# The residual h as eight tiles, operands of the next attention pair ahead of v, four raw weight buffers in the front, caches inside block 0's projections

## The chip, the core and the metric

The kernel runs on one core of a Trainium2 chip. The core has TensorE (PE, matmuls and transposes), VectorE (DVE), ScalarE (ACT), GpSimd (POOL) and SyncE (SP, which here issues every DMA, in one queue and in order). Each engine works its instructions off in the order in which the program has them, and engines wait for one another by semaphores. The metric is the device time of one execution in microseconds; lower is better. The time of a kernel is the median of some runs.

## What is computed

One step of a one-layer encoder over 2048 prompt tokens and 32 sample tokens, D = 1024, all in float32:

```python
z = rmsnorm(h, g_attn) @ w_in                      # 3072 columns: q, k, v of groups A and B
oa = diff_core(qa, ka, va, t5_bias, chunk_mask, lam)  # A: 4 heads, two softmaxes of 64 dims, values of 128
ob = band_core(qb, kb, vb, clip_bias, band_mask)      # B: 8 heads of 64, own chunk and the 8 before
h = h + concat([rmsnorm(oa, subln_g) * 0.8, rmsnorm(ob, out_norm_b)]) @ w_out
c = rmsnorm(h, g_mlp)
h = h + jnp.square(jax.nn.relu(c @ w_up)) @ w_down    # 4096 wide
h = h + jax.nn.sigmoid(h @ w_ple_gate) * (p @ w_ple_proj)
y = rmsnorm(h, g_final)
```

For the 32 sample tokens, keys and values of 128 cached positions (cache_a_k, cache_a_v, cache_b_k, cache_b_v) stand ahead of the new ones. The new keys and values are outputs too.

## The kernel before, in words

**Precision.** A float32 product is made of three fast ones: each operand is split into a high part and the rest (`split`, L194: the high part by ACT or DVE, the rest by POOL or DVE), and `mm3` (L215) issues high·high, high·rest and rest·high. So each weight is loaded raw, cast by ACT and subtracted by POOL (`wunit`, L205). A raw weight takes one of `nraw` buffers of a ring `rawp`; in the front these are two.

**Tokens** stand in four blocks (0 to 3) of 512, 544 (512 and the 32 sample tokens), 512 and 512. Most tensors are kept transposed, 128 features by tokens. What doesn't fit in SBUF is kept in scratch tensors in HBM: qS, kS and vS (split q, k, v), oT (attention's output), hS (the residual h), rS and rB (norms), uS, cS and eS (for the last two blocks' MLP).

**Order of the program** (`run`, L1417). The tile framework allocates buffers, sets all waits and orders the instructions of each engine by a planner: it keeps the program's order as priority and fills an engine's gaps with later work that is ready by its own simulation. Work far behind in the text can so run between earlier work; the MLP of block 0, for instance, fills the gaps of the second attention stage.

1. `prep` of blocks 0 and 1 (norm and transposes), then `proj` (L392): for group A, block 0, then block 1, values first, then q and k for each head pair. Each k tile is also turned back for the output by transposes (`knat`, L478), which wait in a list `late` until the next matmuls of the same call are issued, and at the latest until the end of the call. `setup` (L262) makes the lambda and the bias tables, woven into block 0's projections at steps 0, 8 and 10.
2. `attn_a` (L545) for the query pairs (0, 1), then block 1's projections, `bands`, `caches` (L502: cached keys transposed, split and written to kS, cached values to vS), then the pairs (2, 3) and the sample (8). For each head g a bias tile ba, the keys ka (and ks for the sample) are loaded, then for each pair `attn_a_pair` (L564): q is loaded, scores, softmax, then per four key tiles v is loaded, the weights transposed and multiplied. ba, ka and ks have one buffer in this stage, q and v two.
3. Projections for group B, `attn_b` (L708) of the same form with keys, values and bias loaded per head, and `proj` of blocks 2 and 3 for group A.
4. `weave2` with ONP: the norms of group B's outputs for blocks 0 and 1 (`onorm`) run beside these projections, at steps counted by ONP. Then `attn_a` for the pairs (4, 5) and (6, 7).
5. `outproj` and `cnorm` for blocks 0 and 1, then `mlp` for block 0 and for block 1 (L1556 to L1574): h is loaded from hS into one tile of 8 x 544 columns, each of 16 chunks of the hidden width adds into it (L993), and one DMA stores it to hS at the end (L1574). Beside block 1's MLP runs `side` (L1537): 29 steps in all, `oload` and `outproj` of blocks 2 and 3 (25 with a norm) and four of `xnorm3`, five at a time from chunk 8 on (SIDE).
6. Blocks 2 and 3 together by one step of Strassen's scheme, seven products instead of eight: `uphase` (L1101) with sums of weights ws (L1084) and of activations, then `dphase` (L1177) with weight tiles wd (six buffers). Beside dphase the gates and final norms of blocks 0 and 1 run (`gate`, `final`), behind it those of 2 and 3 (`gatepair`).

At the seam from 5 to 6 the pools of the MLP are closed and those of the up phase are opened in the same part of SBUF: hh (h of blocks 2 and 3), tw (split weights), tr (raw weights), then t2 with 18 buffers, some of which lie where h of block 1 lay.

Of the kernel before, what the change touches and what calls it, by code (L numbers as in the profile page):

```python
# [19 lines left out]
P = 128  # L20
# [63 lines left out]
ONP = (28, 1, 6)  # L84
# [4 lines left out]
SIDE = (8, 5)  # L89
# [70 lines left out]
class Kern:  # L160
    def __init__(self, tc, a):
        self.tc = tc
        self.nc = tc.nc
        self.a = a
        self.nt = 4
        self.nraw = 2

# [94 lines left out]
    def setup(self, cp, wk, ps):  # L262
# [15 lines left out]
        self.rb = self.dram([8, 768], F32, "rb")  # L278
        yield
# [28 lines left out]
        yield  # L308

# [82 lines left out]
    def proj(self, half, grp, acts, sg, mm, tp, vs=range(2), gs=range(4)):  # L392
# [7 lines left out]
        for c in vs:  # L400
# [3 lines left out]
            for b in half:  # L404
                aH, aL = acts[b]
                for c0, n in toks(b):
# [8 lines left out]
                    )  # L415
                    raw = sg.tile([P, 256], F32, tag="vraw", bufs=2, name="vraw")
# [18 lines left out]
        late = []  # L435
        for g in gs:
            gi = 4 * grp + g
            for kind in range(2):
                col = base + 512 * kind + P * g
                wh, wl = self.wunit(W[:, col : col + P].rearrange("(k p) c -> p k c", p=P), [8, P])  # L440
                for b in half:
# [5 lines left out]
                    for s0, n in SUBS[b]:  # L447
# [8 lines left out]
                        while late:  # L456
                            late.pop(0)()
# [38 lines left out]
                    if grp == 0 or b in (1, 3):  # L496
                        late.append(knat)
        while late:
            late.pop(0)()
        yield  # L500

    def caches(self, sg, tp):  # L502
        nc, a = self.nc, self.a
        for grp in range(2):
            nh, dv = (4, 128) if grp == 0 else (8, 64)
            ck = a["cache_a_k"] if grp == 0 else a["cache_b_k"]
            cv = a["cache_a_v"] if grp == 0 else a["cache_b_v"]
            kn = sg.tile([P, 512], F32, tag="kn", bufs=2, name="ckn")
            self.dma(kn, ck)
            tps = tp.tile([P, 4, P], F32, tag="mm", name="ctp")  # L510
            for g in range(4):
                nc.tensor.transpose(tps[:, g], kn[:, P * g : P * g + P], self.ident)
            hi = sg.tile([P, BLK], F32R, tag="qh", bufs=2, name="ckh")[:, :512]
            lo = sg.tile([P, BLK], F32R, tag="ql", bufs=2, name="ckl")[:, :512]
            tf = tps.rearrange("p a b -> p (a b)")
            nc.scalar.activation(hi, tf, AF.Copy)
            nc.vector.tensor_tensor(lo, tf, hi.bitcast(F32), op=ALU.subtract)
            for i, t in enumerate((hi, lo)):
                for g in range(4):
                    self.dma(  # L520
                        self.kS[4 * grp + g, i, :, SP : SP + PAST], t[:, P * g : P * g + P]
                    )
            for c in range(2):
                raw = sg.tile([P, 256], F32, tag="vraw", bufs=2, name="cvr")
                self.dma(raw, cv[:, 256 * c : 256 * c + 256])
                hl = sg.tile([P, nh // 2, 2, dv], F32R, tag="vhl", bufs=2, name="cvhl")
                r3 = raw.rearrange("p (h d) -> p h d", d=dv)
                self.split(hl[:, :, 0], hl[:, :, 1], r3, "dve", "pool")
                self.dma(
                    self.vS[grp][SP : SP + PAST, 512 * c : 512 * c + 512],  # L530
                    hl.rearrange("p a b d -> p (a b d)"),
                )
# [12 lines left out]
    def attn_a(self, js, pool, ps_s, ps_t, ps_o):  # L545
        nc = self.nc
        last = 8 in js
        nk = 256 * (max(j for j in js if j < 8) + 1)
        for g in range(4):
            ba = self.bias_a(pool, g)  # L550
            kt = pool.tile([P, 2, 1024 if self.small else SP], F32R, tag="ka", bufs=1 if self.small else 2, name="ka")
            if last:
                ks = pool.tile([P, 2, PAST + SS], F32R, tag="ks", bufs=1, name="ks")
            for hl in range(2):
                src = self.kS[g, hl].rearrange("(m r) c -> r m c", m=2)
                for c0 in range(0, nk, 1024):
                    c1 = min(c0 + 1024, nk)
                    self.dma(kt[64 * hl : 64 * hl + 64, :, c0:c1], src[:, :, c0:c1])
                if last:
                    self.dma(ks[64 * hl : 64 * hl + 64], src[:, :, SP:KC])  # L560
            for j in js:
                self.attn_a_pair(g, j if j < 8 else None, kt if j < 8 else ks, ba, pool, ps_s, ps_t, ps_o)

    def attn_a_pair(self, g, j, kt, ba, pool, ps_s, ps_t, ps_o):  # L564
# [8 lines left out]
        q = self.load_q(pool, g, t0, nq, (0, 1))  # L573
        ws = []
        for qi, t in enumerate(tiles):
# [132 lines left out]
    def attn_b(self, js, pool, ps_s, ps_t, ps_o):  # L708
        nc = self.nc
# [3 lines left out]
        for h in range(8):  # L713
            gi, m = 4 + h // 2, h % 2
            bb = self.bias_b(pool, h)
            kt = pool.tile([P, KBW], F32R, tag="kb", bufs=2, name="kbt")
            for hl in range(2):
                src = self.kS[gi, hl, 64 * m : 64 * m + 64]
                self.dma(kt[64 * hl : 64 * hl + 64, : ke - kb], src[:, kb:ke])
                if last:  # L720
                    self.dma(kt[64 * hl : 64 * hl + 64, ke - kb : ke - kb + PAST + SS], src[:, SP:KC])
            nv = (ke - kb) // P
            v = pool.tile([P, KBW // P + 1, P], F32R, tag="vb", bufs=2, name="vbt")
            self.dma(
                v[:, :nv],
                self.vS[1][kb : kb + nv * P, P * h : P * h + P].rearrange("(k p) c -> p k c", p=P),
            )
            if last:
                self.dma(v[:, nv], self.vS[1][SP : SP + PAST, P * h : P * h + P])
                self.dma(v[:SS, nv + 1], self.vS[1][SP + PAST : KC, P * h : P * h + P])  # L730
            for j in js:
                if j < 8:
                    self.attn_b_pair(h, j, kt, v, kb, bb, pool, ps_s, ps_t, ps_o)
                else:
                    self.attn_b_pair(h, None, kt, v, SP - (ke - kb), bb, pool, ps_s, ps_t, ps_o)

    def attn_b_pair(self, h, j, kt, v, kb, bb, pool, ps_s, ps_t, ps_o):
# [7 lines left out]
        q = self.load_q(pool, gi, t0, nq, (m,))  # L745
# [4 lines left out]
        for qi, t in enumerate(tiles):  # L750
# [31 lines left out]
            for x0 in range(0, len(kts), 4):  # L782
# [7 lines left out]
                for a0, na, kn in groups:  # L790
# [5 lines left out]
                    nc.vector.tensor_tensor(l_, s_, h_.bitcast(F32), op=ALU.subtract)  # L796
        o = ps_o.tile([P, 256], F32, tag="o", name="ob")
# [165 lines left out]
    def mlp_down(self, ch, nf, blocks, us, st, wk, mm):  # L963
# [3 lines left out]
        for dh in range(nf):  # L967
# [6 lines left out]
            for d in range(nd):  # L974
                dd = nd * dh + d
                for b in blocks:
                    h = st[b][0]
                    for s0, sn in SUBS[b]:
# [13 lines left out]
                        hv = h[:, dd, s0 : s0 + sn]  # L992
# [184 lines left out]
    def dphase(self, h, pool, md):  # L1177
# [35 lines left out]
        for m, sq, so, outs in plan:  # L1213
# [11 lines left out]
            for d in range(4):  # L1225
                for q, op in outs:
                    i, t = int(q[0]) - 1, int(q[1]) - 1
                    hv = h[2 + t][:, 4 * i + d, :512]
# [86 lines left out]
    def gatepair(self, h, up, act, pool, md, mg, lag):  # L1315
# [4 lines left out]
        for b in HALVES[1]:  # L1320
            hs[b] = [act.tile([P, 8, 512], F32R, tag="act", name=n) for n in ("hH", "hL")]
            for i, k in enumerate(order[b]):
                self.split(hs[b][0][:, k], hs[b][1][:, k], h[b][:, k, :], "act", "pool" if i % 4 == 1 else "dve")
        wg, wq = {}, {}
        for i in range(8 + lag):
            for d, b in ((i, 2), (i - lag, 3)):
# [19 lines left out]
                for s0, sn in ((0, 256), (256, 256)) if (d, b) == (7, 3) else ((0, 512),):  # L1346
# [15 lines left out]
                    self.sigate(up, pg, pq, h[b][:, d, t], sn < 512)  # L1362
                yield d, b

    def turned(self, h, c0, tn, q, ps, up, acc):
        nc = self.nc
        yp = ps.tile([P, 512], F32, tag="mm", name="yp")
        for k in range(4):
            nc.tensor.transpose(yp[:tn, P * k : P * k + P], h[:, 4 * q + k, c0 : c0 + tn], self.ident)
# [47 lines left out]
    def run(self):  # L1417
        tc, nc, a = self.tc, self.nc, self.a
        with ExitStack() as top:
# [22 lines left out]
            sg = opened(s12, "sg", 2)  # L1442
            self.consts(cp)
# [229 lines left out]
```

## Time and profile before

| | us |
|---|---|
| median of 3 runs | 3195.66 |
| lowest and highest | 3192.92, 3199.41 |
| the profiled execution | 3189.55 |
| its span, first to last instruction | 3187.7 |
| mean granted clock of TensorE | 0.977 of full |

The profile is of one execution. Busy time counts an engine's own instructions; issue of DMAs and waits are not in it. Waits are put down to what ended last before the waiting instruction started. "L993" is line 993 of the kernel; a tile's name is given as output<-input. A DMA's line is L173 throughout, so its tiles tell which one it is. PE's matmuls overlap, and gaps under some 0.1 us don't show as idle time. The granted clock is full speed or half.

### The profile page before, as it was taken

What the parts mean: (1) busy time and instruction counts of PE and PEld (TensorE: products, weight loads), DVE (VectorE), ACT (ScalarE), POOL (GpSimd) and SP (SyncE); (2) the same over time, 40 slices, a digit from 0 to 9 for tenths busy, and PEclk for the clock granted to TensorE, in tenths of its full rate; (3) what the DMA queues carried; (4) which work ended last, traced back from release to release, by engine and by line L of the source; (5) the groups of instructions that cost most, each with busy time, mean ns of one, the idle gap of its engine ahead of it and who ended that gap; (6) DMA issues with size and microseconds to landing.
All of it is one profiled execution on the core that took longest, in us unless ns stands there. A gap on an engine that the chain in (4) does not pass through costs nothing. (4 is left out here: it accounts for less than half of the span.)

```text
span 3187.7 us, 51326 instructions
## 1 busy us (share of the span) xinstructions
PE 3002.7 (94%) x17399; PEld 2626.0 (82%) x17399; DVE 1785.7 (56%) x4008; ACT 1774.0 (56%) x3809; POOL 1795.1 (56%) x2512
## 2 busy tenths in 40 slices
PE   7898888999999999999999999998799999999997
PEld 6787788889887987888888999888688878878776
DVE  5364655544345545667686652246466665845844
ACT  5465657766566656667676643334244454534454
POOL 7574563543334555556564465667465567767561
PEclk9998999999999999999999999999899999999999
DMA  8986868877777846555555343465544476756721
GB/s 245 285 235 180 226 182 243 245 228 229 215 220 213 240 123 166 159 160 165 146 171 161 104 129 100 152 197 156 166 163 145 145 270 206 243 167 207 245 67 53
DMA packets 566686, 586.15 MB, mean 184 GB/s; under 512 B 42092, under 2 KB 423344, under 8 KB 566424
## 3 DMA queue, kind: packets, MB, share of 16 engines
q1 hardware_dynamic: 566424, 582.87, 60.7%
q8 instruction: 138, 2.26, 0.3%
q14 instruction: 124, 1.02, 0.1%
HBM read 444.66 MB, written 142.01 MB: 184 GB/s over the span
## 5 line engine op out<-in xcount | busy, mean ns | idle before, releaser
L192 POOL TENSOR_TENSOR wl<-wr,wh 128x256 fp32r<-128x256 f32 x824 | 615.6, 778 | 447.6 <-ACT wh L197 380.2
L197 ACT ACTIVATE wh<-wr 128x1024 fp32r<-128x1024 f32 x270 | 285.2, 1057 | 313.9 <-PE dps L220 57.1
L182 POOL TENSOR_TENSOR wl<-wr,wh 128x256 fp32r<-128x256 f32 x256 | 192.5, 783 | 170.1 <-ACT wh L197 170.0
L219 PE MATMUL dps<-uh,wh 128*128 128x272 f32 (+1 forms) x768 | 258.3, 336 | 23.5 <-DVE h L993 19.4
L993 DVE TENSOR_TENSOR h<-h,dps 128x272 f32<-128x272 f32 (+1 forms) x384 | 194.4, 515 | 136.0 <-PE dps L221 134.8
L219 PE MATMUL ups<-cH,wh 128*128 128x272 f32 (+1 forms) x768 | 251.0, 327 | 2.8 <-DVE h L993 2.4
L220 PE MATMUL ups<-cL,wh 128*128 128x272 f32 (+1 forms) x768 | 250.6, 326 | 1.0 <-POOL cL L182 1.0
L221 PE MATMUL ups<-cH,wl 128*128 128x272 f32 (+1 forms) x768 | 251.3, 327 | 0.0
L221 PE MATMUL dps<-uh,wl 128*128 128x272 f32 (+1 forms) x768 | 248.4, 324 | 0.0
L220 PE MATMUL dps<-ul,wh 128*128 128x272 f32 (+1 forms) x768 | 248.3, 323 | 0.0
L219 PE MATMUL qps<-aH,wh 128*128 128x512 f32 (+1 forms) x640 | 229.9, 359 | 4.5 <-DVE a L379 3.0
L221 PE MATMUL qps<-aH,wl 128*128 128x512 f32 (+1 forms) x640 | 228.9, 358 | 0.0
L220 PE MATMUL qps<-aL,wh 128*128 128x512 f32 (+1 forms) x640 | 228.1, 356 | 0.0
L603 PE MATMUL s<-ka,q 128*128 128x512 f32 (+3 forms) x640 | 178.6, 378 | 19.8 <-DMA q<-qS 9.6
L182 POOL TENSOR_TENSOR dw<-dv,dw 128x256 fp32r<-128x256 f32 x160 | 142.8, 920 | 74.3 <-ACT dw L197 69.4
L220 PE MATMUL dp<-dx,dw 128*128 128x512 f32 x448 | 179.2, 400 | 2.3 <-DVE dx L203 2.1
L219 PEld LDWEIGHTS dps<-uh,wh 128*128 128x128 f32 x768 | 145.2, 189 | 43.5 <-DVE h L993 27.9
L219 PE MATMUL dp<-dx,dw 128*128 128x512 f32 x448 | 176.3, 400 | 2.9 <-ACT dx L197 2.9
L221 PE MATMUL dp<-dx,dw 128*128 128x512 f32 x448 | 174.5, 399 | 0.0
L774 DVE CUSTOM_DVE_ANT_0 eb<-sb,bb 128x320 f32<-128x320 f32 (+2 forms) x232 | 103.7, 477 | 112.8 <-PE tpb L786 102.4
L219 PE MATMUL vps<-wh,aH 128*128 128x256 f32 (+1 forms) x544 | 158.1, 293 | 3.6 <-ACT vraw L417 1.6
L609 DVE TENSOR_REDUCE nm<-s 128x1 f32<-128x512 f32 (+1 forms) x192 | 121.0, 639 | 66.8 <-PE s L603 65.9
(275 smaller groups left out, 9550.2 us busy)
## 6 DMA issues: line engine op xcount, KB each, us to landing
wd<-w_down SPq DMA_DIRECT2D x96, 512.0 KB, 5.2
wr<-w_in SPq DMA_DIRECT2D x86, 512.0 KB, 5.3
q<-qS SPq DMA_DIRECT2D x256, 128.0 KB, 4.2
v<-vSa SPq DMA_DIRECT2D x64, 512.0 KB, 4.1
wr<-w_up SPq DMA_DIRECT2D x64, 512.0 KB, 4.2
wr<-w_down SPq DMA_DIRECT2D x64, 512.0 KB, 3.8
ut<-uS SPq DMA_DIRECT2D x56, 512.0 KB, 4.5
ka<-kS SPq DMA_DIRECT2D x32, 512.0 KB, 8.2
```

What stands on the lines that cost most here:

```text
L182: nc.gpsimd.tensor_tensor(out[:, sl], a[:, sl], b[:, sl], op=op)
L192: nc.gpsimd.tensor_tensor(out[:, sl], a[:, sl], b[:, sl], op=op)
L197: nc.scalar.activation(hi, raw, AF.Copy)
L219: nc.tensor.matmul(ps, lh, rh, start=start and i == 0, stop=False)
L220: nc.tensor.matmul(ps, lh, rl, start=False, stop=False)
L221: nc.tensor.matmul(ps, ll, rh, start=False, stop=stop and i == n - 1)
L603: nc.tensor.matmul(s, q[:, m, hl, P * qi : P * qi + nr], kt[:, m, k0 - kb : k0 - kb + n], start=hl == 0, stop=hl == 1)
L609: nc.vector.tensor_reduce(nmx, s, axis=AX.X, op=ALU.max, negate=True)
L774: nc.vector.tensor_tensor_reduce(e[:, w * i : w * i + w], s, bb[:nr, b0 + w * i : b0 + w * i + w], 1.0, -3e38, ALU.add, ALU.max, st[:, 3 + ...
L993: nc.vector.tensor_tensor(hv, hv, ps, op=ALU.add)
```

## The change

`hmove` moves h between SBUF and hS in eight DMAs of one feature tile each; for blocks 0 and 1 h is eight tiles of its own, and the code that indexed `h[:, d]` indexes `h[d]`. At the seam the pool of raw weights (tr) is opened ahead of hh and tw. In both attentions a `fetch(i)` loads what pair i needs (bias, keys, for group B values, and q), and the next pair's fetch is called inside the pair, behind the softmax and ahead of the loads of v; ka has two buffers throughout. In the front `rawp` alternates between two rings of two buffers. `caches` takes one group per call; its four loads are issued in `setup`, and its two calls are steps of `setup`, woven into block 0's projections at steps 0, 6, 8, 10 and 12. The list `late` belongs to the kernel and is emptied behind the next projection's first matmuls, whichever call these are in. ONP begins at 16 instead of 28, SIDE is given chunk by chunk (five steps at chunks 7 to 11, then two, one and one), wd has eight buffers.

```diff
-ONP = (28, 1, 6)
+ONP = (16, 1, 6)
-SIDE = (8, 5)
+SIDE = {**{i: 5 for i in range(7, 12)}, 12: 2, 13: 1, 14: 1}
...
     def setup(self, cp, wk, sg, ps):
...
+        ck, cv = [], []
+        for k, v in ((a["cache_a_k"], a["cache_a_v"]), (a["cache_b_k"], a["cache_b_v"])):
+            ck.append(wk.tile([P, 512], F32, tag=f"ck{len(ck)}", name="ckn"))
+            cv.append(wk.tile([P, 512], F32, tag=f"cv{len(cv)}", name="cvn"))
+            self.dma(ck[-1], k)
+            self.dma(cv[-1], v)
         yield
...
+        for grp in range(2):
+            self.caches(grp, ck[grp], cv[grp], sg, ps)
+            yield
...
     def proj(...):
...
+                    self.flush()
                     raw = sg.tile([P, 256], F32, tag="vraw", bufs=2, name="vraw")
...
-                        while late:
-                            late.pop(0)()
+                        self.flush()
...
-        while late:
-            late.pop(0)()
         yield
+    def flush(self):
+        while self.late:
+            self.late.pop(0)()
...
     def attn_a(self, js, pool, ps_s, ps_t, ps_o):
+        def fetch(i):
+            if i >= len(seq):
+                return
+            g, j = seq[i]
+            if g not in keys:
+                ba = self.bias_a(pool, g)
+                kt = pool.tile([P, 2, 1024 if self.small else SP], F32R, tag="ka", bufs=2, name="ka")
+                ks = pool.tile([P, 2, PAST + SS], F32R, tag="ks", bufs=1, name="ks") if last else None
+                keys[g] = ba, kt, ks
...
+            t0, nq = (TS, SS) if j is None else (tcol(256 * j), 256)
+            got[i] = self.load_q(pool, g, t0, nq, (0, 1))
+        fetch(0)
+        for i, (g, j) in enumerate(seq):
+            ba, kt, ks = keys[g]
+            self.attn_a_pair(
+                g, j, ks if j is None else kt, ba, got.pop(i), lambda: fetch(i + 1), pool, ps_s, ps_t, ps_o
+            )
...
-        q = self.load_q(pool, g, t0, nq, (0, 1))
         ws = []
...
             ws.append(e[0])
+        ahead()
...
+            self.rawp = Rings((self.wp, "wr"), (opened(s12, "rw", 2), "wr"))
...
-                    if i in (0, 8, 10):
+                    if i in (0, 6, 8, 10, 12):
                         next(su)
...
-                        self.caches(sg, tp)
...
+            def hmove(b, h, load):
+                for d in range(8):
+                    x, y = h[d][:, : BN[b]], self.hS[:, d, T0[b] : T0[b] + BN[b]]
+                    self.dma(*((x, y) if load else (y, x)))
                 return h
...
-                h = hload(hq, BLK, b)
+                h = [hq.tile([P, BLK], F32, tag="h", bufs=8, name="h") for _ in range(8)]
+                hmove(b, h, True)
...
-                        for _ in range(SIDE[1] if i >= SIDE[0] else 0):
+                        for _ in range(SIDE.get(i, 0)):
                             next(o, None)
...
-                self.dma(self.hS[:, :, T0[b] : T0[b] + BN[b]], h[:, :, : BN[b]])
+                hmove(b, h, False)
...
+            wr = opened(top, "tr", 1)
             hh = opened(top, "hh", 2)
             self.wp = opened(top, "tw", 1)
-            wr = opened(top, "tr", 1)
...
-            ud = Mix(opened(udx, "dx", 1, side="right"), wd=(ud, 6))
+            ud = Mix(opened(udx, "dx", 1, side="right"), wd=(ud, 8))
```

`attn_b` is changed in the same way as `attn_a`.

More of the change, by code (lines that the diff above doesn't have):

```diff
@@ L166, in __init__ @@
         self.nraw = 2
+        self.late = []
     def dma(self, dst, src):
@@ L496, in proj @@
                     if grp == 0 or b in (1, 3):
-                        late.append(knat)
-        while late:
-            late.pop(0)()
+                        self.late.append(knat)
         yield
[L502 to L510, printed above, removed]
-            for g in range(4):
[L512 to L532, printed above, removed]
@@ new lines, in flush, with caches @@
+    def flush(self):
+        while self.late:
+            self.late.pop(0)()
+    def caches(self, grp, kn, vn, sg, tp):
+        nc = self.nc
+        nh, dv = (4, 128) if grp == 0 else (8, 64)
+        tps = tp.tile([P, 4, P], F32, tag="tp", name="ctp")
+        for g in range(4):
+            nc.tensor.transpose(tps[:, g], kn[:, P * g : P * g + P], self.ident)
+        hi = sg.tile([P, BLK], F32R, tag="qh", bufs=2, name="ckh")[:, :512]
+        lo = sg.tile([P, BLK], F32R, tag="ql", bufs=2, name="ckl")[:, :512]
+        tf = tps.rearrange("p a b -> p (a b)")
+        nc.scalar.activation(hi, tf, AF.Copy)
+        nc.vector.tensor_tensor(lo, tf, hi.bitcast(F32), op=ALU.subtract)
+        for i, t in enumerate((hi, lo)):
+            for g in range(4):
+                self.dma(self.kS[4 * grp + g, i, :, SP : SP + PAST], t[:, P * g : P * g + P])
+        for c in range(2):
+            hl = sg.tile([P, nh // 2, 2, dv], F32R, tag="vhl", bufs=2, name="cvhl")
+            r3 = vn[:, 256 * c : 256 * c + 256].rearrange("p (h d) -> p h d", d=dv)
+            self.split(hl[:, :, 0], hl[:, :, 1], r3, "dve", "pool")
+            self.dma(
+                self.vS[grp][SP : SP + PAST, 512 * c : 512 * c + 512],
+                hl.rearrange("p a b d -> p (a b d)"),
+            )
@@ L738, in attn_b_pair @@
+        fetch(0)
+        for i, (h, j) in enumerate(seq):
+            bb, kt, v = keys[h]
+            self.attn_b_pair(
+                h, j, kt, v, SP - (ke - kb) if j is None else kb, bb, got.pop(i), lambda: fetch(i + 1),
+                pool, ps_s, ps_t, ps_o,
+            )
+    def attn_b_pair(self, h, j, kt, v, kb, bb, q, ahead, pool, ps_s, ps_t, ps_o):
         nc = self.nc
@@ L796, in attn_b_pair @@
                     nc.vector.tensor_tensor(l_, s_, h_.bitcast(F32), op=ALU.subtract)
+        ahead()
         o = ps_o.tile([P, 256], F32, tag="o", name="ob")
@@ L1607, in gates @@
                     yield from self.gate(b, gq, t3, mg)
-                    yield from self.final(b, self.hg, t3, fk, mg)
+                    yield from self.final(b, [self.hg[:, k] for k in range(8)], t3, fk, mg)
             g = gates()
```

103 lines of the change are left out of this document (51 added, 52 removed).

## The prediction

> **What bounds the kernel now.** I read the page first, then the busy time by stage, then TensorE's waits, and last the order of time around the longest of them.
>
> ```profile
> span 3187.7 us, 51326 instructions
> ## 1 busy us (share of the span) xinstructions
> PE 3002.7 (94%) x17399; PEld 2626.0 (82%) x17399; DVE 1785.7 (56%) x4008; ACT 1774.0 (56%) x3809; POOL 1795.1 (56%) x2512
> ```
>
> TensorE (PE) is busy for 94% of the span, and no other engine for more than 56%. The change takes no matmul away, so what it can win is idle time of PE (3187.7 - 3002.7 = 185 us) and time in which its clock was halved. The table by stage tells where that lies (columns: stretch, length, busy time of PE, PEld, DVE, ACT and POOL, granted clock, DMA share, GB/s):
>
> ```profile
> 100.00:420.00 320.00, 280.92 (x1865) 255.00 (x1864) 184.31 (x529) 190.11 (x515) 194.09 (x298) 0.93 0.78 223
> ...
> 2250.00:2300.00 50.00, 28.48 (x129) 23.41 (x129) 19.57 (x23) 14.13 (x25) 22.32 (x27) 0.80 0.61 208
> 2300.00:2600.00 300.00, 300.00 (x1288) 241.72 (x1286) 194.64 (x249) 151.37 (x271) 180.17 (x217) 1.00 0.48 165
> 2600.00:3100.00 500.00, 487.12 (x2329) 401.47 (x2328) 311.36 (x437) 239.60 (x467) 342.73 (x413) 0.99 0.61 200
> ```
>
> The up phase, 2300 to 2600, is full: nothing to win. The front, 100 to 420, leaves PE idle for 39 us and grants 0.93 of the clock. The 50 us from 2250 hold 21.5 us of idleness. Who ended PE's waits, longest in total first (total, times, longest):
>
> ```profile
> PE xps L219 <- ACT wc L1095: 21.5, 1, 21.5
> PE dps L219 <- DVE h L993: 19.4, 23, 3.3
> PE rp L367 <- DVE rsy L233: 14.6, 5, 10.6
> PE s L603 <- DMA q<-qS: 9.6, 5, 4.0
> PE sb L771 <- DVE stb L774: 6.9, 7, 3.1
> PE ktp L482 <- ACT kr L466: 6.7, 2, 6.4
> PE ctp L512 <- DMA ckn<-cache_a_k: 5.6, 1, 5.6
> ```
>
> One wait of 21.5 us, then a tail of small ones. The change aims at rows 1, 2 (in part), 4, 6 and 7. Row 3 is the start of the kernel, which it leaves alone.
>
> **Part 1: the residual h as eight tiles (hmove).** The 21.5 us wait stands between the MLP of block 1 and the up phase. The DMA queue's order of time there, and DVE's:
>
> ```profile
> 2256.14 1.27 SPq L173 DMA_DIRECT2D h<-hS  x2
> 2257.46 4.10 SPq L173 DMA_DIRECT2D hS<-h  x1
> 2275.64 1.77 SPq L173 DMA_DIRECT2D xv<-eS  x4
> ```
>
> ```profile
> 2256.17 0.44 DVE L993 TENSOR_TENSOR h<-h,dps 128x272 f32<-128x272 f32 x1 [0.36 <-PE dps L221]
> 2256.52 0.68 DVE L1084 TENSOR_TENSOR ws<-wq 128x512 f32<-128x512 f32 x1
> 2257.24 0.69 DVE L1084 TENSOR_TENSOR ws<-ws,wq 128x512 f32<-128x512 f32 x1
> 2275.64 0.69 DVE L1084 TENSOR_TENSOR ws<-wq 128x512 f32<-128x512 f32 x1 [17.71 <-DMA hS<-h]
> ```
>
> The last add into h ends at 2256.6. Only then may its store start, for it is one DMA over one tile; it lands at 2275.6. The third weight sum of the up phase writes a buffer of t2 that lies where h lay, so DVE waits 17.71 us, ACT's cast wc and PE behind it. What one store takes, by size:
>
> ```profile
> hS<-hd SPq DMA_DIRECT2D x8, 272.0 KB, 3.7
> tmp<-hS SPq DMA_DIRECT2D x8, 272.0 KB, 4.3
> hS<-h SPq DMA_DIRECT2D x1, 2176.0 KB, 18.2
> ```
>
> With eight tiles, each of 272 KB, a tile is stored when its own last add is done. The 16 last adds stand 0.44 + 0.36 = 0.8 us apart, so the first tile is free some 11 us before the eighth, about 2245; only the eighth waits for 2256.6, if the stores overlap in the queue. It is issued about 0.4 us later and lands 3.7 us on, near 2260.7. Then come two sums of 0.69 us and a cast of 0.6: PE resumes near 2263 instead of 2277.65, a gain of about 15. Without any wait on the store the four sums and the cast alone would end near 2260, a gain of 17 or 18. What may spoil it: the two h loads of 2 MB, issued at 2256.14 ahead of the store. Three transfers of 6.4 MB in 18.2 us are 353 GB/s; if all 4.2 MB still went ahead of the last tile, it would land 12 us later and the gain fall to about 4. In the program the loads come later than the stores, and they are 16 small ones now, so few can pass. **I take -15; ends -4 and -21.5.** Other loads of h (blocks 0 and 1 at the start of their MLP) I cost at nothing, since PE waits there on no row above with h's load; the 8-fold issue (some 0.4 us each) lies beside matmuls.
>
> The Trainium skill speaks against such a split: its page "DMA: Bandwidth & Descriptors", section "Bandwidth", asks for DMAs of 1 MiB and more. By the fixed 2 us and 436 GB/s of its section "Anatomy of one DMA", eight stores done one by one would take some 21 us (an estimate) and land near 2266; no row of this trace shows eight stores of h in flight.
>
> **Part 2: the front (four raw buffers, caches in block 0's projections, late transposes).** The weights' raw buffers are two, and the DMA queue runs in order. Two places show what that does; DMA queue and ACT near 107, and the DMA queue near 250:
>
> ```profile
> 107.13 0.53 SPq L173 DMA_DIRECT2D wr<-w_in  x1
> ```
>
> ```profile
> 115.23 1.06 ACT L197 ACTIVATE wh<-wr 128x1024 fp32r<-128x1024 f32 x1 [12.82 <-DMA wr<-w_in]
> ```
>
> ```profile
> 250.60 5.72 SPq L173 DMA_DIRECT2D q<-qS  x4
> 256.36 0.59 SPq L173 DMA_DIRECT2D wr<-w_in  x1
> 257.00 0.58 SPq L173 DMA_DIRECT2D ckn<-cache_a_k  x1
> ```
>
> ACT stood 12.82 us at a weight cast, the copy kr queued behind it, and PE's transpose ktp behind that (6.4 us). With four raw buffers this load can go out two weights earlier; besides, the transpose is now kept for the next projection's first matmuls (self.late). I credit the whole 6.7. At 257 the cache load ckn goes out just as PE wants it; loaded in setup, long before, its 5.6 us go. The q loads of the next pair are issued before v's and cannot stand behind v's wait for a buffer; I credit half of 9.6, since the 5.72 us at 250 are a wait of q itself, for its own buffer. That is 6.7 + 5.6 + 4.8 = 17.
>
> What comes late instead: caches() issues 20 stores, and its four loads go with it. One of the stores:
>
> ```profile
> L173 SPq DMA_DIRECT2D kS<-ckh x8: 319/426/430, 263.3 to 268.4; - x8
> ```
>
> At 0.43 us each, 24 issues are 10 us of the queue, moved from 171-270 into the stretch before 125, where ka and q of the first attention stage are queued. Matmuls of block 1's projection hide most of it; I charge 4. **Net -13; ends +9 (no wait shortened, the queue time bare) and -27 (all 22, plus 5 us of half clock out of 0.07 x 320 / 0.5 = 45 us spent at half).** The two extra raw buffers take SBUF only.
>
> **Part 3: SIDE.** Block 1's MLP carries the side work of blocks 2 and 3. Its last four steps (xnorm3) fell into one chunk after a wait of DVE, and the h adds queued among them:
>
> ```profile
> DVE xe L1023 <- DMA rl<-rS: 8.0, 1, 8.0
> ```
>
> ```profile
> PE dps L219 <- DVE h L993: 8.0, 7, 2.3
> ```
>
> ```profile
> 2165.00:2192.00 27.00, 18.79 (x123) 16.81 (x122) 26.64 (x40) 10.82 (x19) 21.62 (x22) 0.95 0.57 176
> ```
>
> The first two rows are the waits between 2150 and 2165 and between 2140 and 2195. In the third DVE is busy 26.64 of 27 us: for this stretch DVE is the bound, and PE loses 8.2 us. Now the 29 side steps start one chunk earlier, the four run as two, one and one, and a chunk takes one or two of them beside its 16 adds of 0.44. **I take -7; ends 0 and -11** (with PE's next wait of the same kind and the clock).
>
> **Part 4: wd from 6 to 8 buffers.** In the down phase, when block 1's gate starts, DVE stands at a weight load and the gate's transposed operand stands behind it:
>
> ```profile
> 2814.49 2.39 DVE L1198 TENSOR_TENSOR dv<-wd 128x512 f32<-128x512 f32 x2 [4.74 <-DMA wd<-w_down]
> ```
>
> ```profile
> PE gps L219 <- DVE pT L1253: 3.9, 1, 3.9
> ```
>
> Two more buffers let wd go out before the gate's own loads. **I take -4; ends 0 and -6** (a like wait of dp close by).
>
> **Part 5: fetching ahead in the other attention stages.** Past 420 PE waits on v once, and on q hardly.
>
> ```profile
> PE o L691 <- DMA v<-vSa: 3.7, 1, 3.7
> ```
>
> **I take -1; ends -5 and +10**, the latter from the rival on keys. ONP (norms of blocks 0 and 1 woven in 12 steps earlier) and wr's new place in SBUF I put at nothing: the norm lies beside projections, and the first raw loads of the up phase go out long before the sums at 2256 that read them:
>
> ```profile
> 2227.28 4.65 SPq L173 DMA_DIRECT2D wq<-w_up  x4
> ```
>
> **The sum.** -15 - 13 - 7 - 4 - 1 = -40. The profiled execution took 3189.55 us (span 3187.7), so 3149.5 by its own measure; the median of the runs is 6.1 higher, which gives **3156 us** (3195.66 - 40).
>
> **The rivals.**
>
> *The front gives nothing.* In 100-420 the DMA share is already 0.78 and DVE, ACT and POOL are each busy for some 190 of the 320 us, so another of them is soon last; then waits only change their names and the 24 issues cost 5. Against it: ckn and ktp have one clear cause each. Time: -15 - 7 - 4 + 5 = -21, 3175 us.
>
> *The stores don't free the tiles early.* If h loads still go ahead, or the eight stores run one by one (8 x 3.7 = 30 us from 2245, landing near 2275), part 1 gives 0 to 4 and the change does there not what it says. Time 3195.66 - 27 = 3169. [...] For it: the 18.2 us. Against it: 18.2 us for three transfers is a rate, not a latency.
>
> *Keys ahead of v makes it slower.* fetch() of a new head in group A first loads ba, which has one buffer and waits until the running pair has read its bias, then up to 2 MB of keys; v of the running pair now stands behind all that in the queue.
>
> ```profile
> 1666.56 4.12 SPq L173 DMA_DIRECT2D ka<-kS  x4
> ```
>
> ```profile
> ka<-kS SPq DMA_DIRECT2D x32, 512.0 KB, 8.2
> ```
>
> There are four stages of four heads, so 12 such changes of head. At 6 us each (between the 4.12 of issue and the 8.2 of landing) they cost 72 and the change ends at 3228; from 40 / 12 = 3.3 us each on it is slower. For it: the queue is in order. Against it: at 1666 the planner already sends the keys before v, PE lost only 3.7 us, and it fills such places with projection and MLP matmuls.
>
> *It cancels.* The planner places all work anew, and waits like row 5 (6.9 us) grow as others go: 3196.
>
> **How the numbers follow.** Forecast 0.56, front gives nothing 0.16, stores not early 0.10, keys ahead of v 0.08, cancels 0.08, still faster than 3130 (most terms at their far end) 0.02. The range 3130 to 3188 takes in the first three with the inner part of their terms' ends (0.82). A measurement of this kernel tells about 0.2% (6.4 us) from no change: faster 0.84, same 0.08, slower 0.08.
>
> **What would show it.** Right: the row xps <- ACT wc under 8 us; eight hS<-h issues, the first before 2250; no wait of PE on ckn; ktp below 2; dps <- DVE h between the last chunks under 3 instead of 8; gps <- DVE pT gone. Wrong: xps still above 15; new rows of o <- v above 10 in total; the idle time of the front (39 us) unchanged; the queue full past 125 with PE waiting for ka or q.

## The result and the profile after

| | before | changed |
|---|---|---|
| median, us (runs) | 3194.46 (4) | 3160.20 (4) |
| lowest and highest | 3192.92, 3199.41 | 3158.11, 3162.07 |
| profiled execution, span | 3189.55, 3187.7 | 3162.07, 3160.3 |

The ratio is 0.9898, 95% interval 0.9882 to 0.9914: 34 us faster by the medians, 27 to 38 by the interval (here and below the ratio is not that of the medians, so the two can differ by a few us). Run again beside the last experiments it was 0.9911, 0.9894 to 0.9928. The time, 3160, lies near the 3156 that were forecast. The gains do not lie where the prediction put them.

The head of the changed kernel's page, and its table by stage (columns as in the prediction):

```profile
span 3160.3 us, 51390 instructions
PE 2995.1 (95%) x17399; PEld 2618.5 (83%) x17399; DVE 1775.7 (56%) x4008; ACT 1775.2 (56%) x3809; POOL 1806.6 (57%) x2512
```

```profile
100.00:420.00 320.00, 282.28 (x1919) 256.35 (x1918) 186.48 (x537) 195.08 (x528) 194.44 (x297) 0.96 0.78 221
2250.00:2300.00 50.00, 46.80 (x199) 37.10 (x199) 26.98 (x37) 28.73 (x52) 38.40 (x48) 1.00 0.69 234
```

The 50 us from 2250 now keep PE busy for 46.8 us instead of 28.5. The front has hardly moved: 282.3 busy instead of 280.9. Who ended PE's waits in the changed kernel:

```profile
PE dps L220 <- DVE h L1020: 17.9, 27, 2.3
PE rp L377 <- DVE rsy L234: 15.9, 5, 10.6
PE vps L220 <- ACT vraw L428: 7.3, 5, 4.4
PE sb L797 <- DMA q<-qS: 7.1, 2, 4.1
PE s L617 <- DMA ka<-kS: 7.0, 1, 7.0
PE dp L221 <- DVE dx L204: 6.2, 5, 2.6
PE s L617 <- DMA q<-qS: 6.1, 4, 2.2
PE xps L220 <- ACT wc L1122: 5.3, 1, 5.3
```

The 21.5 us of xps are 5.3. The cached keys (ckn) and the kr wait of ktp have left the list, but v's copy (vps, 7.3) and the keys (ka, 7.0) have come into it, and dps, which the SIDE table was to relieve, stands at 17.9 after 19.4.

**Where the time went.** Start times can't be compared late in a kernel that has shifted as a whole. So PE's matmuls are counted as work: each by the usual issue interval of its shape (20th percentile in the trace of before), 2770 us in all. A stretch is the time between two sums of work, the same two in every kernel, and the table gives each stretch's length in before's trace and how much longer or shorter it is in the others. It is computed from the traces; the stretches are named by their time in before. Two stretches where nothing beyond 2 us happened are left out.

```
kernel (traces)          11-659 659-773 883-1007 1007-1903 1903-2233 2233-2358 2664-3096
before, length            648.8   114.2    124.7     895.4     330.5     124.8     432.0
changed                    -5.2    +6.8    -13.1      +2.1      -1.2     -12.4      -6.7
changed again (e12)        -6.3    +8.7    -12.8      +2.2      +0.7      -5.9      -6.6
e1 eight tiles             +0.7    -0.1     -0.1      +0.1      -2.5     -14.5      -2.1
e2 eight tiles, tr first   +2.5     0.0     +0.7      +2.2      -1.4      -9.6      +0.3
e3 front                   -8.5    +8.4     +3.3      +5.1      -1.9      +2.1      -1.9
e4 fetching ahead          -6.6    -0.5     -1.0      +0.1      -2.9      +1.4      -3.1
e9 ONP                     +3.5    -0.5     -9.2      -2.3      -3.6      +1.2      -1.1
e5 changed, tr back        -9.8    +9.3    -12.2      +3.5      -2.1     -14.8      -6.5
e6 changed, wd 6           -3.9    +9.7    -12.5      +6.4      -2.6     -11.0      -2.3
e7 changed, old SIDE       -1.5    +6.6    -12.0      +5.3      -2.1      -9.3      -6.1
e8 changed, no fetching    -9.4    +7.9    -11.9      +0.5      -2.3     -12.0      -6.4
e11 changed, ACT, raw 2    +1.9    +3.2     -7.7      -6.4      +0.4     -12.6      -8.6
e10 before + four parts    -6.7    -0.2    -12.1      -7.6      -2.9     -13.1      -6.1
```

How far to trust it: in the first column changed, e12, e5, e6 and e7 have the same program and differ by 8.3 us; in the second by 3.1; at the seam (2233-2358) changed and e12 differ by 6.5. Only what separates whole groups of rows is read below.

### The profile page after: what moved, and what is told of

It is laid out like the page before. It is cut to its first block, busy times and chain, and to the rows that moved or that the text cites. A ratio compares the mean times of both kernels' runs of the same rounds, so it can differ in the third digit from the quotient of the medians.

```text
span 3160.3 us, 51390 instructions
## 1 busy us (share of the span) xinstructions
PE 2995.1 (95%) x17399; PEld 2618.5 (83%) x17399; DVE 1775.7 (56%) x4008; ACT 1775.2 (56%) x3809; POOL 1806.6 (57%) x2512
## 5 line engine op out<-in xcount | busy, mean ns | idle before, releaser
L193 POOL TENSOR_TENSOR wl<-wr,wh 128x256 fp32r<-128x256 f32 x824 | 622.1, 787 | 462.8 <-ACT wh L198 395.8
L183 POOL TENSOR_TENSOR wl<-wr,wh 128x256 fp32r<-128x256 f32 x256 | 194.2, 790 | 167.7 <-ACT wh L198 166.3
L220 PE MATMUL dps<-uh,wh 128*128 128x272 f32 (+1 forms) x768 | 259.6, 338 | 23.8 <-DVE h L1020 17.9
L221 PE MATMUL vps<-wl,aH 128*128 128x256 f32 (+1 forms) x544 | 159.2, 294 | 0.3 <-POOL wl L193 0.3
L222 PE MATMUL vps<-wh,aL 128*128 128x256 f32 (+1 forms) x544 | 157.9, 291 | 1.2 <-POOL aL L193 1.2
```

The source lines that it names most:

```text
L183: nc.gpsimd.tensor_tensor(out[:, sl], a[:, sl], b[:, sl], op=op)
L193: nc.gpsimd.tensor_tensor(out[:, sl], a[:, sl], b[:, sl], op=op)
L220: nc.tensor.matmul(ps, lh, rh, start=start and i == 0, stop=False)
L221: nc.tensor.matmul(ps, lh, rl, start=False, stop=False)
L222: nc.tensor.matmul(ps, ll, rh, start=False, stop=stop and i == n - 1)
```

## The experiments

Times are medians of the runs; ratios are to the kernel before on the same chip, with 95% intervals. e1 to e4 ran on one chip, e5 to e8 on a second, e9 to e12 on a third.

**e1: only the eight tiles** (hmove and h as eight tiles put into the kernel before; the pool tr stays behind hh and tw).

> The kernel before with h as eight tiles and nothing else (the raw-weight pool keeps its place). Theory, that the seam's wait is the one store of h: xps <- ACT wc falls from 21.5 to about 6 us and the kernel is 15 to 19 us faster; all before the seam is as in the kernel before. Rival, that the h loads of 4.2 MB go ahead of the last stores or the stores run one by one: xps stays above 15 and the gain is under 5 us.

3179.58 us, 0.9956 (0.9941 to 0.9971). The gain stands in one column, -14.5 at the seam, where PE's wait on wc is 3.9 us instead of 21.5.

**e2: the eight tiles and the new place of tr.**

```diff
+            wr = opened(top, "tr", 1)
             hh = opened(top, "hh", 2)
             self.wp = opened(top, "tw", 1)
-            wr = opened(top, "tr", 1)
```

> As the first, and the raw-weight pool opened ahead of h's pool as in the changed kernel. Theory, that the place of the raw pool is worth nothing: the same time as the first kernel within 3 us. Rival, that the new place is what makes the first up-phase weights late or early: a difference of 5 us or more, with the first wq issue moved by as much.

3188.86 us, 0.9977 (0.9963 to 0.9992): 9 us behind e1 by the medians, and less is left at the seam, -9.6. The first wq goes out at 2255.08 instead of 2226.01 in e1. The DMA queue at the seam, in e1:

```profile
2226.01 4.55 SPq L173 DMA_DIRECT2D wq<-w_up  x4
2242.22 12.67 SPq L173 DMA_DIRECT2D hS<-h  x7
```

the same in the changed kernel, and DVE's first sum of weights there:

```profile
2234.15 7.17 SPq L174 DMA_DIRECT2D hS<-h  x7
2241.43 0.39 SPq L174 DMA_DIRECT2D wq<-w_up  x1
2241.91 0.67 SPq L174 DMA_DIRECT2D hS<-h  x1
2242.67 3.82 SPq L174 DMA_DIRECT2D wq<-w_up  x3
```

```profile
2248.52 0.75 DVE L1111 TENSOR_TENSOR ws<-wq 128x512 f32<-128x512 f32 x1 [6.77 <-DMA wq<-w_up]
```

In e1 the four weight loads of the up phase are issued 16 us ahead of the stores and no sum waits for them. With tr in its new place they come behind seven of the eight stores and DVE stands for 6.77 us.

**e3: only the front** (four raw buffers, caches in setup, late transposes), the rest as before.

> The kernel before with four raw buffers, the caches in block 0's projections and the transposes kept over the end of a call; no other part. Theory of the prediction: waits on ckn and on kr (12.3 us) go and the kernel is 8 to 13 us faster, and the gain still stands at the first matmul of the output projection. Rival, that the front is bound by other work and waits change their names: 0 to 3 us, PE as idle in 100-420 as before (39 us).

3191.85 us, 0.9988 (0.9976 to 0.9999): some 4 us instead of the 8 to 13. It gains 8.5 us in the first column (between 100 and 420 PE is idle for 31 us instead of 39) and gives 8.4 back in the next.

**e4: only fetching ahead**, in both attentions.

> The kernel before with the next pair's operands fetched ahead of v in both attentions, ka with two buffers; no other part. Theory: waits of PE on q shrink by half (9.6 to 5), 1 to 6 us faster. Rival of keys ahead of v: new waits on v or ka of 10 us and more in total, no gain or slower.

3180.54 us, 0.9950 (0.9935 to 0.9965). It gains 6.6 in the first column, the same place as the front, and gives nothing back. That is more than the 1 to 6 us that were expected (16 by the medians), and it did not come by the way that was expected, since PE's waits on q have hardly shrunk:

```profile
PE s L615 <- DMA q<-qS: 8.4, 5, 4.0
```

What has shrunk are the waits that the front aims at: between 95 and 140 ACT's longest wait for a raw weight is 6.9 us instead of 12.8, PE's wait of ktp on kr is 0.3 instead of 6.7, and the one on ckn 2.8 instead of 5.6.

**e5: the changed kernel with tr behind hh and tw again** (e2's edit undone).

> The changed kernel with the pool of raw weights opened behind h's pool and the split weights' again, as in the kernel before; nothing else. Theory from the first two runs, that the new place makes the first four wq loads of the up phase wait behind the stores of h: they go out some 15 us ahead of the stores again, the first xps matmul comes before the last dps, and the kernel is 4 to 10 us faster than the changed one (near 3153). Rival, that in the changed kernel the seam's end is set by the loads of h ahead of xv anyway: the same time within 3 us.

3166.34 us, 0.9912 (0.9889 to 0.9935); the total tells nothing, for this chip scattered more (before from 3184.68 to 3210.26). The seam does: -14.8. With the tiles and tr behind, the seam gives -14.5, -14.8 and -13.1 (e1, e5, e10), mean -14.1; with tr first -12.4, -5.9, -9.6, -11.0, -9.3 and -12.0 (changed, e12, e2, e6, e7, e8), mean -10.0. No value of the one group lies in the other, though the groups come within 0.7 us. By the means the new place costs about 4 us. DVE's wait for wq goes with it throughout: 6.8 to 7.1 us in these six, none in the three. PE's own wait on wc is 5.3 to 5.7 us against 3.7 to 3.9, so this row shows under 2 of the 4.

**e6: the changed kernel with six wd buffers.**

```diff
-wd=(ud, 8)
+wd=(ud, 6)
```

> The changed kernel with six buffers for wd. Theory of the prediction: gps <- DVE pT (3.9 us) is back, the stage from the start of the down phase to the end is 4 to 6 us longer, and all before it is as in the changed kernel. Rival, that this gain came with the new schedule and not with the buffers: under 2 us.

3171.94 us, 0.9930 (0.9905 to 0.9955). In the last column every kernel with eight buffers lies between -6.1 and -8.6, every one with six between +0.3 and -3.1. In e6 PE waits for the gate's operand again (PE's waits from 2760 to 2900):

```profile
PE gps L220 <- DVE pT L1280: 2.5, 1, 2.5
```

The row is absent in all seven kernels with eight buffers and stands at 2.0 to 3.9 us in the seven with six, before among them. The buffers are worth some 5 us.

**e7: the changed kernel with the old side steps** (five from chunk 8 on).

> The changed kernel with the side work of blocks 2 and 3 from chunk 8 on, five steps at a time, as before. Theory of the prediction: dps <- DVE h near the end of block 1's MLP grows by 5 to 8 us and the kernel is slower by as much. Rival, from the changed kernel's own trace, where these waits still are about 9 us: no difference within 3 us.

3167.73 us, 0.9912 (0.9888 to 0.9936). Block 1's MLP, 1903-2233: -2.1, beside -1.2 and +0.7 for the changed kernel. The new table of SIDE gives nothing. PE's waits between 2100 and 2195 in the changed kernel:

```profile
PE dps L220 <- DVE h L1020: 7.2, 7, 2.3
```

That is the row that was to go from 8.0 to under 3; in e12, the same program, it is 5.4, and with the old side steps it is 4.6.

**e8: the changed kernel without fetching ahead.**

> The changed kernel with attention as before (q and keys fetched at the start of each pair and head, ka with one buffer in the first stage). Theory from the fourth run, that fetching ahead is worth some 15 us: slower by 10 to 18 us, lost in the first attention stage, before 420. Rival, that the four raw buffers and the moved caches already unblock the queue there, so that both gains are one and the same: slower by under 5 us.

3157.94 us, 0.9889 (0.9868 to 0.9910): no slower. What fetching ahead gives alone (e4), it doesn't give beside the front: the first column is -9.4 without it and -1.5 to -9.8 with it.

**e9: only ONP**, 16 instead of 28 in the kernel before.

> The kernel before with one number changed: ONP begins at 16 instead of 28. Theory, from the earlier runs (every kernel with ONP at 16 gains some 12 us between the same two sums of matmul work, those reached at 883 and 1007 us of the kernel before, and no kernel with ONP at 28 does): the stored norm rB of block 0 is issued near 880 instead of 967, so that the output projection can fill PE beside group B's last pairs; the stretch gains 10 to 13 us, elsewhere nothing beyond 4 us either way, total -8 to -12 (ratio 0.9962 to 0.9975). Rival (the prediction's zero: the norm lies beside projections, and the 12 us come from fetching ahead in group B or from the planner's new placing): 0 within 4 us in that stretch, ratio 0.999 to 1.001.

3178.84 us, 0.9956 (0.9940 to 0.9971): one number is worth 18 us by the medians and 14 by the ratio; in the trace 9.2 of it lie between 883 and 1007. Every kernel with 16 gains 7.7 to 13.1 in that column, and of those with 28 none gains more than 1.0. The norm's store and load in before, the first operand of the output projection that needs this norm, and PE there:

```profile
967.00 0.54 SPq L173 DMA_DIRECT2D rB<-r  x1
969.84 0.33 SPq L173 DMA_DIRECT2D rb<-rB  x1
```

```profile
973.54 0.63 ACT L197 ACTIVATE oact<-oraw 128x512 fp32r<-128x512 f32 x1 [1.32 <-DVE oraw L853]
```

```profile
950.00:990.00 40.00, 31.87 (x155) 26.39 (x156) 28.70 (x87) 29.07 (x60) 7.27 (x14) 0.87 0.66 190
```

and PE in the same 40 us of e9 and of the changed kernel:

```profile
950.00:990.00 40.00, 36.51 (x191) 30.47 (x190) 25.74 (x68) 26.41 (x50) 17.11 (x24) 0.96 0.82 232
```

```profile
950.00:990.00 40.00, 38.79 (x210) 32.39 (x209) 25.08 (x69) 26.64 (x52) 16.26 (x25) 1.00 0.93 269
```

Block 0's output projection takes eight operands. The four from group A are there by 952.7 in before, and PE works with them from 958.5 to 964.5. The four from group B need the norm and come from 973.54 on; the projection goes on at 975.2. From 965 to 975 PE runs group B's last pairs alone and is busy for 5.25 of the 10 us. In the 40 us it is idle for 8.1 us at a granted clock of 0.87. In e9 the norm is stored at 880.7, in the changed kernel at 882.1, and the fifth operand is there at 960.8 and 964.2; PE is busy for 7.2 and 10.0 of the same 10 us, and the granted clock of the 40 us is 0.96 and 1.00.

**e10: before with four parts only**: the eight tiles (tr behind), fetching ahead, ONP at 16, wd at eight. Without the front, the new SIDE and the new place of tr.

> The kernel before with the eight tiles (the pool tr behind hh and tw, as before), fetching ahead, ONP at 16 and wd at eight; the front (two raw buffers, caches between the stages, late transposes per call) and SIDE as before. Theory that the front and SIDE give nothing and tr's new place costs 4: -14.7 at the seam, -12 by ONP, -4 to -7 by wd and the gate, and a few us of fetching ahead in the front, so -32 to -40 in all, ratio 0.9875 to 0.990, not slower than the changed kernel. Rival (front and SIDE carry their predicted 13 and 7): -20 or less, ratio above 0.9937.

3142.82 us (3139.93 to 3153.28), 0.9837 (0.9819 to 0.9856). That is a larger gain than the 32 to 40 us that were expected, and faster than the changed kernel, which took 3170.67 (3156.81 to 3173.01) on the same chip. It lacks the front's +6.6 to +9.7 in the second column, has -13.1 at the seam, and -7.6 in 1007-1903, where of its parts fetching ahead and the tiles of block 0's h work, which alone have +0.1 each there (e4, e1). e11, with two raw buffers too, has -6.4 there, and the kernels with four have +0.5 to +6.4; so the front may cost something there as well, but the cause stays open. The page and the waits of this kernel:

```profile
PE 2987.2 (95%) x17399; PEld 2614.6 (83%) x17399; DVE 1780.0 (57%) x4008; ACT 1772.2 (56%) x3809; POOL 1792.8 (57%) x2512
```

```profile
PE dps L219 <- DVE h L1018: 15.5, 23, 2.6
PE rp L367 <- DVE rsy L233: 13.8, 4, 10.6
PE tpp L690 <- DVE e L654: 8.7, 6, 5.8
PE s L615 <- DMA q<-qS: 8.7, 5, 3.4
```

ka is not among the waits, though this kernel fetches ahead too.

**e11: the changed kernel with the stores of h on ScalarE's DMA queue, and two raw buffers in the front.**

```diff
-                    self.dma(*((x, y) if load else (y, x)))
+                    if load:
+                        self.dma(x, y)
+                    else:
+                        nc.scalar.dma_start(y, x)
...
-            self.rawp = Rings((self.wp, "wr"), (opened(s12, "rw", 2), "wr"))
```

> The changed kernel with two edits that lie 1500 us apart and are read where they lie. (a) The eight stores of h are issued by ScalarE's queue and no longer by SyncE's. Theory that the up phase's first weight loads only stand behind these stores in SyncE's queue: the first four wq go out before 2232, DVE's first sum of weights waits under 1 us instead of 6.77, and PE's wait of 5.3 us on the cast wc goes below 2; the seam gains another 3 to 6 us. Rival (ScalarE stands at the stores until VectorE's last adds, and the casts behind it are as late; or the tiles' release is what counts): wait of 4 us or more, no gain. (b) Two raw buffers in the front instead of four. If the second ring is worth its predicted share, PE's transposes ktp wait some 6 us again and the work reached by 770 us of the kernel before comes 5 us or more later than in the changed kernel; if not, within 4 us.

3162.66 us, 0.9894 (0.9878 to 0.9909). (a) The theory fell. DVE's wait for wq and ACT's for the last adds, in e11:

```profile
2249.10 0.69 DVE L1111 TENSOR_TENSOR ws<-wq 128x512 f32<-128x512 f32 x1 [4.58 <-DMA wq<-w_up]
```

```profile
2236.92 7.97 ACTq L1567 DMA_DIRECT2D hS<-h  x8
2244.95 1.15 ACT L1122 ACTIVATE wc<-wq 128x512 fp32r<-128x512 f32 x2 [15.73 <-DVE h L1020]
```

With no store in SyncE's queue, one wq goes out at 2224.77, but the second only at 2244.07, and DVE's sum still waits 4.58 us; besides, ACT now stands at the stores. So the queue had held back the first load alone. At the second, SyncE's queue now waits in one piece for 18.8 us on PE's dps, a matmul of block 1's down projection: it is the buffer that is not free. The addresses in the compiled program say why: in e11, with tr first, the second and third wq lie where split weights wh of block 1's down projection lie, which PE reads until the last chunk; in e10, with tr behind, the first, third and fourth lie over cL, free since the last up projection, and the second over a relu tile that is free from then as well. PE's waits on wc are 2.6 us instead of 5.3, but waits on Xt have grown from 3.2 to 3.9, and the seam is no shorter (-12.6 after -12.4). (b) With two raw buffers the first column has +1.9 instead of -1.5 to -9.8 (PE's wait on kr is back, 4.9 us, at the matmuls qps), and the second loses 3.2 instead of 6.6 to 9.7. By 773 e11 is 3.5 and 2.7 us behind the two traces of the changed kernel, and so within the 4 us that were set for a ring that is not worth its share: what the second ring wins first, it largely loses behind. The other two edits of the front, the moved caches and the late transposes, were not run apart from each other.

**e12: the changed kernel again**, beside e9 to e11.

> The changed kernel once more, unaltered, on the same chip as the three others, so that they stand beside it: ratio 0.988 to 0.992 to the kernel before. It also gives how far two profiled executions of one program differ at the same place: within 4 us if the shifts of 10 us and more that the other runs were read by are to stand.

3170.67 us, 0.9911 (0.9894 to 0.9928). Three columns of two traces of this one program agree within 0.3 us, the seam differs by 6.5 against the 4 that were asked. Taken with the 8.3 us of the first column, this says that a shift below some 8 us in a single trace carries nothing.

## Why the prediction was right, and which of its steps failed

The sum of -40 met -34. By its terms, sizes read from the groups of the table:

| term | predicted | measured | from |
|---|---|---|---|
| part 1, eight tiles | -15 | -14 | e1, e5, e10 |
| tr's new place | 0 | +4 | e2, e6, e7, e8 against these |
| part 2, front | -13 | about 0 in the two first columns | e3; e11 |
| part 3, SIDE | -7 | 0 | e7 |
| part 4, wd | -4 | -5 | e6, and all with eight against all with six |
| part 5, fetching ahead | -1 | alone -7 in the first column (-13 by its span), 0 beside the front | e4, e8 |
| ONP | 0 | -9 alone, -8 to -13 in all with 16 | e9 and all with 16 |

**Part 1 held, with its working.** The stores overlap, the first is issued at 2234.15, 7.6 us before the last add ends (2241.75), and a store of 272 KB lands soon, though most of them have others in flight beside them:

```profile
hS<-h SPq DMA_DIRECT2D x8, 272.0 KB, 2.1
```

The last column is 2.1 us at the median, beside 18.2 for the one store before. The rival that the stores free nothing early is out. The rule of the Trainium skill, "DMA: Bandwidth & Descriptors", section "Bandwidth", to make DMAs of 1 MiB and more, is about the share of peak bandwidth, measured on loads issued from GpSimd. It did not decide here: eight stores of 272 KB were 14 us better than one, because of when they could start. A slip in this part's bound changed nothing: 12 us later than 2263 is 2275, a gain of under 3 us and not of 4.

**The zero for tr's place failed.** The prediction said that the first raw loads go out long before the sums that read them. That was read from a trace in which tr lay over buffers whose last use was long past; moved to the front of the area, two of its four buffers lie over split weights that PE reads to the end, and their loads wait for that. A pool's place decides whose last reader its first writer waits for.

**Part 2's waits went, its gain did not.** ckn and ktp's 6.4 us are gone as written, and the first column gained. But of the rivals "the front gives nothing" came true for this part, and for its reason: waits changed their names. Two of the prediction's own signs against it are there. In the changed kernel PE is idle for 37.7 us between 100 and 420, after 39.1. And PE waits for ka (the row of 7.0 us) and for q, whose waits went from 8.7 to 3.9 us between 100 and 420, but from 0.3 to 7.1 between 420 and 660. The wait for ka is 6.8 to 8.0 us in the five kernels with the whole front and fetching ahead, 3.8 in e8, and absent in e3, e4, e10 and e11. It is not shown to come from the issues that were moved forward: half of these keys goes out at 205.07, as the store of their low part (kS<-ql, issued at 199.81) lands, and lands at 210.44, when PE starts. And behind the first column comes the loss of 7 to 10. What stands there, ACT in the changed kernel and in e10:

```profile
690.12 0.60 ACT L821 ACTIVATE pHb<-tpb 128x512 fp32r<-128x512 f32 x1
696.32 0.66 ACT L861 ACTIVATE oraw<-oraw 128x544 f32<-128x544 f32 x1 [5.61 <-DMA oraw<-oT]
697.00 0.38 ACT L843 ACTIVATE t<-ob 64x256 f32<-64x256 f32 x1
```

```profile
702.55 0.66 ACT L859 ACTIVATE oraw<-oraw 128x544 f32<-128x544 f32 x1 [2.08 <-DMA oraw<-oT]
```

The norm's square stands in ACT's order ahead of its load's landing, and the copy t queues behind it. DVE and then PE, in the changed kernel:

```profile
697.42 0.42 DVE L844 TENSOR_TENSOR t<-ob,t 64x256 f32<-64x256 f32 x1 [5.05 <-ACT t L843]
```

```profile
698.17 0.45 PE L812 MATMUL tpb<-ident,eb 128*128 128x128 f32 x1 [4.13 <-DVE stb L804]
```

DVE waits 5.05 us for that copy, and PE's transposes 4.13 us for DVE's next reduction. In the six other kernels with four raw buffers ACT waits there 5.2 to 7.4 us in one piece, in six with two (before, e1, e2, e4, e9, e10) at most 3.4; e11, with two, waits 6.0 and loses half as much. So the chain is seen, and that the front's new placing puts it there fits; no run took this wait alone away, and it isn't shown to be the whole of the loss.

**Part 3 failed in its premise.** DVE at 26.64 of 27 us was taken for the bound of PE's waits. Spread over more chunks, the waits stayed (7.2 and 5.4 us in two traces, after 8.0), and with the old steps under the new code they were 4.6: they come from the chunk's own adds, or from what the planner puts there; which, stays open.

**Part 4 came in its size.** The row gps <- DVE pT is gone with eight buffers. The way that was given for it, DVE standing at wd, is shown only in part: DVE's waits for wd are 1.8 us in the changed kernel after 9.5, but 8.9 in e10, which gains as much.

**ONP's zero failed in a word.** "The norm lies beside projections" is true of the norm, but its result gates half the operands of an output projection, and without them PE had nothing to run beside group B's last pairs. PE's waits from 880 to 1010 in before:

```profile
PE sb L771 <- DVE stb L774: 4.7, 3, 3.1
PE tpb L786 <- DVE pLb L796: 3.6, 3, 2.4
```

They read like waits of the softmax; they show where other matmuls were missing. In e9 the first row is 0.6 us and the second is absent; a wait of 3.3 us of the output projection on its own operands has come.

**Part 5's sum was mis-placed.** Half of q's waits in the front had been credited to the front's part. But fetching ahead alone left these waits (8.4 us after 9.6) and removed those of ktp and in part of ckn, for which the front had been credited 12.3: the two take the same time, they are not additive, and the sum added them. Why fetching ahead shortens the wait for the raw weight stays open. (The 5.72 us at 250, which the prediction put down to q's own buffer, stand in the trace as waits of the queue on landings of ka, 3.3, and v, 2.0.) The rival, keys ahead of v, did not come: PE's wait on v is 0.2 us after 3.7.

So 20 us of parts 2 and 3 did not come and tr's place took 4, ONP brought some 13 that were not counted, and parts 1 and 4 came in their size. By the spans the change brought 27.4 us, by the medians 34, beside 40 forecast. That the total came near is in good part luck: errors cancelled.

## What to carry to other kernels

Ask of every step that is moved what its result releases, and not only what it lies beside: a norm that was late kept out the matmuls that fill PE's gaps. Two edits that remove waits of the same stretch are not to be added; each is to be run alone, and left out alone: four of the seven parts here give 54 us by the medians, all seven give 26 on the same chip. Before a pool is moved, see whose last reads lie at its new addresses.

## What the runs showed of the hardware

Eight stores of 272 KB, most of them issued 0.8 us apart as their tiles became free, landed 2.1 us after issue at the median, while one store of 2176 KB beside two loads of h took 18.2. Executions of one program differ in places more than expected: by 8.3 us in the first column, over five traces, and by 6.5 us at the seam, with PE's longest wait there nearly equal (5.3 and 5.4 us).
